# A retention stage with gelu's table loaded earlier, gelu in halves, and three more fixed places in the engines' queues

## The chip, the cores and the metric

One core of a Trainium2 chip runs the kernel. The metric is the device time in microseconds, from several runs; beside them stands one execution taken by the hardware profiler, whose trace has every instruction of the engines (TensorE or PE, its weight loads PEld, VectorE or DVE, ScalarE or ACT, GpSimd or POOL, SyncE or SP) with start and duration. Times inside the trace are counted from the start of the span.

## The reference

A trunk of two layers on x of 1 x 1024 x 1024 in float32. Layer 0 projects the normed x once and feeds an S5 branch and a retention branch; layer 1 is a convolution module.

```python
# layer 0
u_s5, g_s5, q, k, v, g_ret = split(rmsnorm(x) @ w_in)
y = gelu(s5(u_s5)); y = y * sigmoid(y @ glu_w + glu_b)       # S5 branch with its GLU
y_s5 = y * silu(g_s5)
y_ret = retention(rope(q) / 8, rope(k), v) * silu(g_ret)     # 8 heads, normed per head
x = x + concat(y_s5, y_ret) @ w_out
# layer 1
a, b, g = split(rmsnorm(x) @ w_in_c)
u = layernorm(conv31(a * sigmoid(b)))
x = x + (silu(u) * silu(g)) @ w_out_c
return rmsnorm(x)
```

## The kernel before

Everything is held transposed: 128 rows of features by tokens, the 1024 tokens in two halves h of 512. A float32 product is made of three matmuls (`mm3`, L224): each operand is split into a high part, rounded to fp32r, and a low part, the rest. Weights pass through `wload_pieces` (L209): a DMA on SP loads wf, ScalarE casts it to wh (L220), GpSimd or VectorE subtracts to get wl (L221). Each of the three has three buffers, and `wnext` (L162) asks for two weights ahead of the one in use. Some weights are used twice; their low part is then stored and loaded again (`wload_again`, L191).

The order of the instructions on each engine isn't that of the program text. The kernel is built with a timeline planned ahead: an instruction takes its place on its engine when the plan sees its operands ready and the engine free, and the one traced first has precedence. The engines then run these queues strictly in order; SP's queue of DMA issues too. Three means set the order by hand: `issue_after(ins)` puts the instructions of a block behind `ins` on the engine of `ins`; `at(priority)` changes the precedence; and the pairs of `ORDER` (L41) and `s5_order` (L49) put one named instruction behind another on one engine. A pair ('DVE', ('kraw_3', 0), ('yn_2', 0)) reads: on VectorE, the first instruction that writes kraw_3 stands behind the first that writes yn_2.

Retention (`retention`, L1077) goes over four pairs of heads. For each, `ret_proj` projects k and q on PE (mm_k, mm_q) and turns them: four DMAs swap rows of 32 into swp, GpSimd makes two products for each half (L1158, L1160), VectorE adds them (L1161). V comes from `ret_values_wide` for pairs 0 and 1 together (PE mm_v, L1216 to L1218, eight weights v0_0_0 to v0_1_3 in the order h, j, whose low halves GpSimd makes) and from `ret_values` for pairs 2 and 3: eight blocks, each in one of three PSUM banks and copied from there by ScalarE (L1195). `ret_heads` then makes the scores, the state and the output, and norms it per head: VectorE's statistics, a root on ScalarE (`last_rs`, L530, four for each pair), the reciprocal.

Beside each pair k, `y_pass` (L1027) takes two blocks of the S5 branch's output y through gelu: it loads yt (tile yp, one buffer), ScalarE computes the gelu of 128 x 1024 into yn, reading yt with a stride (L1038), SP stores yn, and VectorE forms sums and differences of its quadrants (L1046 to L1049) and splits them for the GLU, whose product is made of seven smaller ones. From pair 1 on the gelus stand behind the last root of the pair before; in pair 2 also behind the copies of V's third and last blocks. `glu_sums` (L1058) forms the same sums of the GLU's weights in the buffers swp and raw that retention frees, and stores them. The root's function and gelu are in different activation tables of ScalarE, so a table load stands between them; in the kernel before nothing names it, and it appears in the trace ahead of the activation that needs it (L1038, L530).

The GLU follows in `layer0_back_and_layer1` (L1343): products mm_glu on PE, and for each block a VectorE operation into a spare bank (mm_gluy, L1460, for half 0; mm_gluz, L1477, for half 1), then `gated` (L1403): tanh on ScalarE in that bank, and VectorE's multiplication with yg (L1421), the second operation on mm_gluy or mm_gluz. For half 1 the bank that L1477 reads is then the target of the next product (y22). After this come w_out (mm_wo, with yr0 and yr1 loaded and split by `load_split`), layer 1's products, its convolution (VectorE's taps, L1626) and w_out_c (mm_oc, `w_out_c`, L1770). There, blocks 0, 1 and 2 of half 1 begin while the normed and gated z comes row block by row block from `conv_scale`. Each such block is 24 matmuls into one bank, three for each row block: number 0 is high by high of row block 0, number 2 the first that needs the weight's low part, number 6 the first that needs row block 2.

Of the kernel before, what the change touches and what calls it, by code (L numbers as in the profile page):

```python
# [14 lines left out]
AF = mybir.ActivationFunctionType  # L15
# [4 lines left out]
P = 128  # L20
# [21 lines left out]
    ('DVE', ('kraw_3', 0), ('yn_2', 0)),  # L42
    ('SP', ('gs1_3', 0), ('t_d', 7)),
    ('DVE', ('cv6_0', 23), ('h1l0_1', 0)),
    ('Pool', ('qswp_0', 0), ('wl_v0_0_1', 0)),
)


# [53 lines left out]
class Trunk:  # L102
# [924 lines left out]
    def y_pass(self, rp, k):  # L1027


        nc = self.nc  # L1030
        yns = []
        for i, cb in enumerate((k, k + 4)):
            yt = rp.tile([P, 8, P], F32, name=f"yp_{cb}", tag="yp", bufs=1)
            nc.sync.dma_start(yt[:], self.y_d[cb].rearrange("i h g m -> (h g) i m"))
            yn = rp.tile([P, P, 8], F32, name=f"yn_{cb}", tag="ynt", bufs=2)

            with self.tc.issue_after((self.last_v if i else self.third_v).ins) if k == 2 else nullcontext():
                nc.scalar.activation(yn[:], yt[:].rearrange("p i m -> p m i"), AF.Gelu_apprx_tanh)  # L1038
            yn = yn[:].rearrange("p m i -> p (m i)")
            nc.sync.dma_start(self.yn_d[cb * P:(cb + 1) * P], yn)  # L1040
            yns.append(yn)
        (b11, b12), (b21, b22) = ((y[:, :HALF], y[:, HALF:]) for y in yns)
        v = nc.vector
        yield
        with self.tc.issue_after(self.last_raw.ins):
            v.tensor_tensor(b22, b22, b12, op=ALU.subtract)  # L1046
            v.tensor_tensor(b12, b12, b11, op=ALU.subtract)
            v.tensor_tensor(b11, b22, b11, op=ALU.add)
            v.tensor_tensor(b21, b11, b21, op=ALU.subtract)  # L1049
        yield  # L1050
        for i in range(2):
            hi = rp.tile([P, T], F32R, name=f"th{i}_{k}", tag="yp", bufs=1)
            v.tensor_copy(hi[:], yns[i])
            v.tensor_tensor(yns[i].bitcast(F32R), yns[i], hi[:].bitcast(F32), op=ALU.subtract)
            nc.sync.dma_start(self.t_d[i, 0, k * P:(k + 1) * P], hi[:].bitcast(F32))
            nc.sync.dma_start(self.t_d[i, 1, k * P:(k + 1) * P], yns[i])
# [20 lines left out]
    def retention(self, st):  # L1077
        nc, A = self.nc, self.A
        rp = self.rp = self.pool("ret", 1, stack=st)
        early = ExitStack()  # L1080
        rq = self.rq = self.pool("retq", 1, stack=early, side="right")
        self.rk = rq.tile([P, 2, T], F32, name="ropek")
        nc.sync.dma_start(self.rk[:], A["rope_k"])
        self.g128 = rp.tile([P, 4], F32, name="g128")
        nc.sync.dma_start(self.g128[:], A["ret_g128"])
        ahead = None
        for pair in range(4):
            cur = list(ahead or self.ret_proj(pair))[-1]

            ahead = pair == 1 and self.ret_proj(pair + 1)  # L1090
            if ahead:
                next(ahead)
            for g, tag in (((0, "swp"), (1, "raw")), (), ((3, "raw"),), ())[pair]:
                self.glu_sums(g, tag)
            if pair == 0:
                V = self.ret_values_wide()
            elif pair > 1:
                V = self.ret_values(pair)
            with ExitStack() as held:
                if pair:  # L1100
                    held.enter_context(self.tc.issue_after(self.last_rs.ins))
                parts = self.y_pass(rq, pair)
                next(parts)
                if pair != 2:
                    next(parts)
                if pair in (0, 3):
                    next(parts, None)

            def scored():

                if pair == 2:
                    with self.tc.issue_after(self.masked[0].ins):
                        next(parts)

            def turned():
                if pair == 3:
                    early.close()
                    self.lp = self.pool("l1", side="right")
            self.ret_heads(pair, *cur, V, turned, scored)

            if pair < 3:
                with self.tc.issue_after((self.ons[0] if pair in (1,) else self.masked[1]).ins):
                    if pair == 0:
                        self.glu_sums(2, "swp")
                    else:
                        next(parts, None)
# [892 lines left out]
```

## Time and profile before

| | before |
|---|---|
| device time, median of 3 runs | 1135.58 us (1133.12 to 1136.41) |
| profiled execution | 1138.03 us |
| its span in the trace | 1136.2 us |
| retention with y's gelus | about 317 to 560 us |
| GLU of S5 | about 529 to 627 us |
| w_out_c of half 1 | from about 1081 us |
| granted TensorE clock, mean | 0.999 |

A timeline row has start, duration, engine, line, operation, output <- input, shape and count; in brackets the idle time of the engine before it and what ended it. A row with x2 or x3 merges neighbours, its duration from the first's start to the last's end. A row of waits has the total, how often, and the longest. PE rows of one matmul are about 0.4 us long but follow each other every 0.2, since matmuls are pipelined.

### The profile page before, as it was taken

What the parts mean: (1) busy time and instruction counts of PE and PEld (TensorE: products, weight loads), DVE (VectorE), ACT (ScalarE), POOL (GpSimd) and SP (SyncE); (2) the same over time, 40 slices, a digit from 0 to 9 for tenths busy, and PEclk for the clock granted to TensorE, in tenths of its full rate; (3) what the DMA queues carried; (4) which work ended last, traced back from release to release, by engine and by line L of the source; (5) the groups of instructions that cost most, each with busy time, mean ns of one, the idle gap of its engine ahead of it and who ended that gap; (6) DMA issues with size and microseconds to landing.
All of it is one profiled execution on the core that took longest, in us unless ns stands there. A gap on an engine that the chain in (4) does not pass through costs nothing.

```text
span 1136.2 us, 17205 instructions
## 1 busy us (share of the span) xinstructions
PE 1117.1 (98%) x6278; PEld 978.9 (86%) x6278; DVE 828.1 (73%) x1470; ACT 498.0 (44%) x731; POOL 647.3 (57%) x456
## 2 busy tenths in 40 slices
PE   9999999999999999999999999999999999999997
PEld 7888888888888889898888888888888888888886
DVE  6973966777417469587569632599999899999734
ACT  6412433333223221323436523555535677446773
POOL 2059999888127344232475011589544568779863
PEclk9999999999999999999999999999999999999999
DMA  9345555553477866959998998565778755357965
GB/s 354 114 124 167 188 185 176 177 172 138 151 245 251 303 212 181 337 168 325 382 372 277 328 330 285 192 237 198 242 252 281 249 195 179 119 179 246 317 229 187
DMA packets 118181, 262.51 MB, mean 231 GB/s; under 512 B 10704, under 2 KB 42320, under 8 KB 117456
## 3 DMA queue, kind: packets, MB, share of 16 engines
q1 hardware_dynamic: 114640, 248.82, 64.9%
q10 hardware_dynamic: 3456, 12.58, 2.8%
q8 instruction: 49, 0.80, 0.3%
q14 instruction: 36, 0.29, 0.1%
HBM read 182.53 MB, written 74.65 MB: 226 GB/s over the span
## 4 chain that ended last, share of the span: by engine, by line
PE 73%; DMA 13%; DVE 7%; ACT 3%; issue 2%; POOL 1%; SPq 1%; POOLq 0%; DVEq 0%; ACTq 0%
PE mm_g L231 7%; PE mm_g L232 7%; PE mm_g L233 7%; PE mm_wo L231 5%; PE mm_wo L233 5%; PE mm_wo L232 5%; PE mm_a L233 2%; DMA yp<-y_d 2%; PE mm_b L232 2%; PE mm_a L231 2%; PE mm_b L233 2%; PE mm_a L232 2%; PE mm_b L231 2%; PE mm_oc L233 2%; PE mm_oc L231 2%; PE mm_oc L232 2%
## 5 line engine op out<-in xcount | busy, mean ns | idle before, releaser
L1626 DVE SCALAR_TENSOR_TENSOR cv<-u,convw,cv 128x512 f32<-128x512 f32 x390 | 267.7, 749 | 5.4 <-ACT cv L1593 3.4
L1587 POOL TENSOR_TENSOR tp<-tp,tp 128x512 f32<-128x512 f32 x64 | 82.4, 1288 | 33.8 <-ACT tp L1586 32.9
L231 PE MATMUL mm_g<-xh,wh_g 128*128 128x512 f32 x256 | 97.9, 382 | 0.0
L232 PE MATMUL mm_g<-xl,wh_g 128*128 128x512 f32 x256 | 97.0, 379 | 0.0
L233 PE MATMUL mm_g<-xh,wl_g 128*128 128x512 f32 x256 | 95.7, 379 | 0.0
L492 POOL TENSOR_TENSOR s1q<-s1q,s1q 128x512 f32<-128x512 f32 x12 | 17.1, 1424 | 79.1 <-ACT s1q L487 79.1
L1586 ACT ACTIVATE tp<-u,convw 128x512 f32<-128x512 f32 x64 | 45.3, 718 | 34.4 <-POOL tp L1587 33.6
L231 PEld LDWEIGHTS mm_g<-xh,wh_g 128*128 128x128 f32 x256 | 48.8, 191 | 6.8 <-issue 0.2
L442 DVE TENSOR_TENSOR gt<-mm_g,R 128x512 f32<-128x512 f32 x32 | 21.9, 686 | 44.7 <-PE mm_g L233 44.6
L233 PEld LDWEIGHTS mm_g<-xh,wl_g 128*128 128x128 f32 x256 | 48.4, 189 | 6.9
L232 PEld LDWEIGHTS mm_g<-xl,wh_g 128*128 128x128 f32 x256 | 48.4, 189 | 6.6
L221 POOL TENSOR_TENSOR wl_glu<-wf_glu,wh_glu 128x1024 fp32r<-128x1024 f32 x14 | 34.0, 2432 | 33.1 <-ACT wh_glu L220 33.1
L233 PE MATMUL mm_oc<-zh,wl_woc 128*128 128x512 f32 (+1 forms) x144 | 51.0, 357 | 1.2 <-DMA wl_woc<-lo_woc 1.2
L232 PE MATMUL mm_oc<-zl,wh_woc 128*128 128x512 f32 (+1 forms) x144 | 51.2, 356 | 0.0
L231 PE MATMUL mm_oc<-zh,wh_woc 128*128 128x512 f32 (+1 forms) x144 | 50.7, 363 | 0.0
L232 PE MATMUL mm_u<-xl,wh_u 128*128 128x512 f32 x128 | 48.3, 381 | 0.7 <-DVE xl L365 0.7
L233 PE MATMUL mm_a<-h1h,wl_ca 128*128 128x512 f32 x128 | 48.6, 380 | 0.3 <-DMA wl_ca<-lo_ca 0.3
L231 PE MATMUL mm_wo<-ysh,wh_wos 128*128 128x512 f32 x128 | 48.9, 382 | 0.0
L231 PE MATMUL mm_g<-h1h,wh_cg 128*128 128x512 f32 x128 | 48.9, 382 | 0.0
L232 PE MATMUL mm_wo<-ysl,wh_wos 128*128 128x512 f32 x128 | 48.5, 379 | 0.0
L233 PE MATMUL mm_wo<-ysh,wl_wos 128*128 128x512 f32 x128 | 48.5, 379 | 0.0
L233 PE MATMUL mm_b<-h1h,wl_cb 128*128 128x512 f32 x128 | 48.5, 379 | 0.0
(533 smaller groups left out, 3601.9 us busy)
## 6 DMA issues: line engine op xcount, KB each, us to landing
wf_g<-w_ab SPq DMA_DIRECT2D x16, 512.0 KB, 5.0
wf_wos<-w_out SPq DMA_DIRECT2D x16, 512.0 KB, 4.5
wf_wor<-w_out SPq DMA_DIRECT2D x16, 512.0 KB, 5.6
wf_cb<-w_c SPq DMA_DIRECT2D x16, 512.0 KB, 4.8
wf_ca<-w_c SPq DMA_DIRECT2D x16, 512.0 KB, 5.6
wf_woc<-w_out_c SPq DMA_DIRECT2D x16, 512.0 KB
wf_v<-w_v SPq DMA_DIRECT2D x12, 512.0 KB
wf_cg<-w_c SPq DMA_DIRECT2D x11, 512.0 KB, 4.5
```

Source lines behind the costliest of these rows:

```text
L221: self.low_made = lo[i].tensor_tensor(wl[:].rearrange(fl)[:, c], wf[:, c], h.bitcast(F32), op=ALU.subtract)
L231: nc.tensor.matmul(ps, wh[:, kb, :], xh, start=start, stop=False, **more)
L232: nc.tensor.matmul(ps, wh[:, kb, :], xl, start=False, stop=False, **more)
L233: self.last_mm = nc.tensor.matmul(ps, wl[:, kb, :], xh, start=False, stop=stop, **more)
L442: nc.vector.tensor_tensor(nat(gt[:, c]), un(ps[:]), nat(self.R[:, c]), op=ALU.mult)
L492: nc.gpsimd.tensor_tensor(a, a, sq[:], op=ALU.add)
L1586: nc.scalar.mul(sk[:], u[:, k:k + HALF], cw[:, nb, k:k + 1])
L1587: gp.tensor_tensor(s0[:], s0[:], sk[:], op=ALU.add)
L1626: v.scalar_tensor_tensor(dst[:], *tap, accs_[i][:], op0=ALU.mult, op1=ALU.add)
```

## The change

Five edits. The pair on GpSimd puts the first product of pair 0's swapped q (L1160, qswp_0) behind the low half of weight v0_1_0 instead of that of v0_0_1, which is three weights later. A new pair on PE puts the third matmul of mm_oc2_1_0 (w_out_c, block 2, half 1) behind the seventh of mm_oc0_1_0. A new pair on VectorE puts the second operation on mm_gluy3 (L1421) behind the first on mm_gluz0 (L1477). For pairs 1, 2 and 3 a load of gelu's table is issued behind the last root of the pair before. And in these pairs each gelu of 128 x 1024 becomes two, for output columns 0 to 63 and 64 to 127 of the outer index (512 elements each).

```diff
@@ ORDER
-    ('Pool', ('qswp_0', 0), ('wl_v0_0_1', 0)),
+    ('Pool', ('qswp_0', 0), ('wl_v0_1_0', 0)),
+    ('PE', ('mm_oc2_1_0', 2), ('mm_oc0_1_0', 6)),
+    ('DVE', ('mm_gluy3', 1), ('mm_gluz0', 0)),
 )
@@ y_pass
             with self.tc.issue_after((self.last_v if i else self.third_v).ins) if k == 2 else nullcontext():
-                nc.scalar.activation(yn[:], yt[:].rearrange("p i m -> p m i"), AF.Gelu_apprx_tanh)
+                for m in ((slice(0, 64), slice(64, P)) if k in (1, 2, 3) else (slice(0, P),)):
+                    nc.scalar.activation(yn[:, m], yt[:, :, m].rearrange("p i m -> p m i"), AF.Gelu_apprx_tanh)
@@ retention
                 if pair:
                     held.enter_context(self.tc.issue_after(self.last_rs.ins))
+                    nc.scalar.preload_act_table_set("gelu_apprx_tanh_and_others")
                 parts = self.y_pass(rq, pair)
```

## The prediction

> **What bounds the kernel now.** I read the page first, then the waits of TensorE (PE) from 300 to 660 us, then the timelines of the engines around each wait.
>
> ```profile
> PE 1117.1 (98%) x6278; PEld 978.9 (86%) x6278; DVE 828.1 (73%) x1470; ACT 498.0 (44%) x731; POOL 647.3 (57%) x456
> ...
> PE 73%; DMA 13%; DVE 7%; ACT 3%; issue 2%; POOL 1%; SPq 1%; POOLq 0%; DVEq 0%; ACTq 0%
> ```
>
> PE is busy 98% of the span and carries 73% of the chain that ended last. So the end moves only by what PE's idle gaps gain or lose. Between 300 and 660 us these are its waits (columns: total us, times, longest):
>
> ```profile
> PE mm_glu L231 <- ACT sg L1416: 1.6, 1, 1.6
> PE mm_v L1217 <- POOL wl_v L221: 1.5, 2, 1.2
> PE mm_v L1192 <- ACT v L1195: 1.1, 1, 1.1
> PE mm_glu L231 <- ACT v L1195: 0.9, 1, 0.9
> PE mm_wo L231 <- ACT yr0h L1339: 0.9, 1, 0.9
> PE mm_glu L231 <- DVE mm_gluz L1477: 0.7, 1, 0.7
> PE mm_k L233 <- POOL wl_k L221: 0.6, 1, 0.6
> ```
>
> The five edits each stand at one such gap: the GpSimd place at mm_v <- wl_v (1.2), the table and the halves at the two gaps <- ACT v (1.1 and 0.9), the VectorE place at mm_gluz (0.7), the TensorE place at one more gap near the end (1.2, shown below). Together that is 5.2 us, the most that the gaps aimed at can give. The three others (sg, yr0h, wl_k) are not touched and can take gains back, since PE will reach them earlier.
>
> **The change part by part.**
>
> *1. GpSimd: the q swap multiplies behind the low half of v0_1_0.*
>
> ```profile
> 350.46 2.51 POOL L1160 TENSOR_TENSOR qswp<-qswp,ropeq 128x512 f32<-128x512 f32 x2 [1.40 <-DMA gs<-w_glu]
> ```
>
> ```profile
> 352.93 8.36 POOL L221 TENSOR_TENSOR wl_v<-wf_v,wh_v 128x1024 fp32r<-128x1024 f32 x3
> ```
>
> ```profile
> 348.72 1.05 ACT L220 CAST wh_v<-wf_v 128x1024 fp32r<-128x1024 f32 x1 [1.15 <-issue]
> ```
>
> GpSimd stood idle 1.40 us, from 349.06, waiting for the swapped q, then spent 2.51 on it, and only at 352.93 began the low halves that PE was about to need: three in 8.36, of which the first (v0_0_3) is PE's wait of 1.2. Its cast and that of v0_1_0 (ended 349.77) were done. Put ahead, two lows run from 349.06 at about 2.4 each, so that v0_0_3 is ready near 351.5 and the 1.2 goes. What moves back: two multiplies, from 350.46 to about 353.8, and with them the q additions on VectorE, the load of gs into the buffer that they free, and what stands behind that load in SP's in-order queue, up to the next K weights:
>
> ```profile
> 351.77 4.51 DVE L1161 TENSOR_TENSOR qrot<-qrot,qswp 128x512 f32<-128x512 f32 x2 [6.12 <-POOL qswp L1160]
> 356.20 2.87 DVE L1046 TENSOR_TENSOR yn<-yn,yn 128x512 f32<-128x512 f32 x1
> ```
>
> ```profile
> 362.37 0.68 DVE L1048 TENSOR_TENSOR yn<-yn,yn 128x512 f32<-128x512 f32 x1
> ```
>
> ```profile
> 372.78 1.11 SPq L218 DMA_DIRECT2D wf_k<-w_ab  x1
> ```
>
> The same kind of VectorE operation takes 0.68 alone and 2.87 where a GpSimd operation runs beside it, so it is held for some 2.2. I walk the queue by that: swaps from 353.8 to 356.4, the q additions done near 357.6 instead of 356.28 (351.77 + 4.51), so 1.4 later; then the sums of y and gs, of which one or two fewer meet a low half (2.2 to 4.4 saved) but which wait for the later gs load (1.4) and may meet the next low half instead (2.2 lost). The chain ends between 2 us earlier and 0.7 later. The wf_k load at 372.78 stands in SP's queue behind the stores of those sums, and PE already waits 0.6 for its low half, so what PE has won is kept only as far as wf_k comes earlier. Ends: 1.8 (the 1.2 and the 0.6 both go) and minus 0.7. I take **1.0**, nearer the upper end, because buffers for weights also come free sooner as the low halves end sooner.
>
> A rule that speaks against this edit: GPSIMD Engine Reference of the Trainium skill (section 1, Specifications) says that GpSimd's SBUF interfaces are shared with VectorE, with contention for VectorE instructions that have two SBUF inputs. The trace agrees (0.68 alone, 2.87 beside GpSimd). By the rule alone the delayed additions and sums meet whatever low halves are left, the first rival, and the sum would be 2.3 instead of 4.0.
>
> *2. The table behind the preceding pair's last root; gelu in halves.* In pair 1 nothing is to be had, since the load already follows the root at once (405.33):
>
> ```profile
> 404.75 0.56 ACT L530 ACTIVATE rs<-mv,epst 128x4 f32<-128x4 f32 x2
> 405.33 1.28 ACT L1038 ACT_TABLE_LOAD   x1
> ```
>
> In pair 2 it isn't so:
>
> ```profile
> 456.49 0.47 ACT L1195 ACTIVATE v<-mm_v,Rtok 128x256 f32<-128x256 f32 x1 [2.21 <-PE mm_v L1194]
> ```
>
> ```profile
> 460.40 0.47 ACT L1195 ACTIVATE v<-mm_v,Rtok 128x256 f32<-128x256 f32 x1 [3.43 <-PE mm_v L1194]
> 465.84 1.28 ACT L1038 ACT_TABLE_LOAD   x1 [4.97 <-DMA yp<-y_d]
> 467.14 1.98 ACT L1038 ACTIVATE yn<-yp 128x1024 f32<-128x1024 f32 x1
> 469.02 1.19 ACT L1195 ACTIVATE v<-mm_v,Rtok 128x256 f32<-128x256 f32 x3
> ```
>
> ```profile
> 469.53 0.38 PE L1192 MATMUL mm_v<-wh_v,xh 128*128 128x256 f32 x1 [1.13 <-ACT v L1195]
> ```
>
> ScalarE copied V block 3 (460.40), then waited 4.97 for yp, loaded the table (1.28), ran the gelu (1.98), and only then copied three finished blocks. PE has three banks for them and stood 1.13. With the table loaded before, the gelu begins at 465.84. Two halves cost a little more than one: a 1024-wide cast is 1.05 (348.72) and a 512-wide one 0.57 (1083.10, below), so 0.09 per cut, six cuts on ScalarE, which is 44% busy. The stores of yn stay one per block, so no DMA is added. The copies then start near 467.9 (465.84 + 1.98 + 0.09) instead of 469.02, or near 466.9 if one is placed between the halves. The wait falls to 0.1 or to nothing: **1.05**, ends 1.13 and minus 1.6 (the third rival). Unhidden, the table load has only been moved: where it now runs, ScalarE is waiting for V blocks (2.21 idle before 456.49). If a copy stood right behind it there, it would be up to 1.28 late, still less than the slack of two free banks at 2.68 (2.21 + 0.47) each.
>
> In pair 3:
>
> ```profile
> 498.68 0.56 ACT L530 ACTIVATE rs<-mv,epst 128x4 f32<-128x4 f32 x2 [3.96 <-DVE mv L1316]
> 500.15 1.28 ACT L1038 ACT_TABLE_LOAD   x1 [0.91 <-DMA yp<-y_d]
> 501.44 2.05 ACT L1038 ACTIVATE yn<-yp 128x1024 f32<-128x1024 f32 x1
> 508.69 2.05 ACT L1038 ACTIVATE yn<-yp 128x1024 f32<-128x1024 f32 x1 [5.21 <-DMA yp<-y_d]
> ```
>
> ```profile
> 528.39 0.62 ACT L1339 CAST y21h<-y21f 128x512 fp32r<-128x512 f32 x1 [6.08 <-DMA y21f<-yn_d]
> 528.92 0.83 ACT L1195 ACTIVATE v<-mm_v,Rtok 128x256 f32<-128x256 f32 x2
> ```
>
> ```profile
> 529.44 0.48 PE L231 MATMUL mm_glu<-y11h,wh_glu 128*128 128x512 f32 x1 [0.94 <-ACT v L1195]
> ```
>
> The roots end at 499.24, yp is there at 500.15. The load can run from 499.24 to 500.52, so the first gelu begins 0.92 earlier, less 0.09 for the cut. The second yp is loaded into the buffer that the first gelu frees, then come the second gelu, yn, y11, y21, and y21's cast (528.39) ahead of the two copies for which PE waits 0.94. All of this is one chain of DMA and engines with little idle time of its own, so the 0.8 arrives: **0.8**, ends 0 (y21 held elsewhere) and 0.94.
>
> *3. VectorE: mm_gluz0 ahead of mm_gluy3's second operation.*
>
> ```profile
> 599.20 0.69 DVE L1425 SCALAR_TENSOR_TENSOR ysl<-mm_gluy,ysh 128x512 fp32r<-128x512 f32 x1
> 600.09 0.70 DVE L1421 SCALAR_TENSOR_TENSOR mm_gluy<-mm_gluy,yg 128x512 f32<-128x512 f32 x1 [0.20 <-ACT mm_gluy L1416]
> 600.70 0.69 DVE L1477 TENSOR_TENSOR mm_gluz<-gu,mm_glu 128x512 f32<-128x512 f32 x1
> ```
>
> ```profile
> 610.00:620.00 10.00, 10.00 (x48) 8.77 (x47) 10.00 (x11) 5.04 (x9) 4.41 (x3) 1.00 0.82 276
> ```
>
> The product into that bank waits for the addition that ends at 601.39. From 599.89 VectorE was free for it, so it ends near 600.5 and the 0.7 goes; the displaced operation comes 0.4 later, and so do what it feeds on ScalarE and the buffer it frees for a yg load. Some 25 us on, PE waits 0.9 for yr0h, whose loads need VectorE, full in that stretch (10.00 of 10). PE's lead may be spent there. Ends 0.72 and minus 0.4; I take **0.4**.
>
> *4. TensorE: the third product of mm_oc2 behind the seventh of mm_oc0.*
>
> ```profile
> 1083.10 0.57 ACT L1339 CAST zh<-zz 128x512 fp32r<-128x512 f32 x1
> ```
>
> ```profile
> 1085.31 0.48 PE L233 MATMUL mm_oc<-zh,wl_woc 128*128 128x512 f32 x1 [1.24 <-DMA wl_woc<-lo_woc]
> ```
>
> PE is held at 1085.31 by the low weights of block 2, while z of row block 2 is there since 1083.67 (its low part some 0.7 later). Products of blocks 0 and 1 with it can run first, at 0.21 each (48 in 10.00). One is certain, two are likely (0.43), all six would fill 1.24. Ends 0.2 and 1.24, **0.75** taken. Behind the pinned product only products of PE queue, and all are wanted before the same bank reads.
>
> The sum: 1.0 + 1.05 + 0.8 + 0.4 + 0.75 = **4.0 us**. The profiled execution took 1138.03 (span 1136.2, 1.8 around it), so it would become 1134.0. It lies 2.45 above the median of 1135.58; brought to that median, the forecast is **1131.6**.
>
> **The rivals.**
>
> *First edit given back at K.* The additions are held behind other low halves and wf_k leaves 0.7 later. Against it: fewer operations stand beside GpSimd. Sum 4.0 minus 1.7 = 2.3: **1133.3**.
>
> *Slower: the same hold, twice more.* Place: VectorE between 353.8 and 372, before SP's wf_k. Price: 2.2 for each further operation held. With two, wf_k leaves 0.7 + 4.4 = 5.1 later and PE's lead elsewhere (3.0) doesn't pay for it: 2.1 slower, **1137.7**. It decides from wf_k 3.0 later, 375.8 in today's times. For it: all of this is in one in-order queue. Against it: GpSimd has then fewer low halves left.
>
> *The table edit doesn't do what it says.* The order of each queue is planned ahead, and the plan misjudged yp by the 4.97 above. If the gelu is planned ahead of block 3's copy, or the load lands in front of the gelu again, part 2 gives nothing or less: without them 4.0 minus 1.85 = 2.15, **1133.4**; with block 3 blocked too, PE stops a block (2.68) sooner and, the copies coming 1.1 sooner, the gap grows by 1.6 instead of falling by 1.05: 4.0 minus 2.65 = 1.35, **1134.2**.
>
> **How the numbers follow.** Forecast 0.60 (its own range 1130.0 to 1133.2), given back at K 0.15, table edit without effect 0.13, slower by the hold 0.12. The range goes from 1129.8 (all 5.2 and the 0.6 at K) to 1135.6, and leaves out the slower case and tails. About 0.3%, 3.4 us, is what a measurement of this kernel can tell from no change, so faster needs below 1132.2: some 0.75 of the forecast and a little of the rest, 0.47. Slower needs above 1139.0: the far half of the hold and an order worsened elsewhere, 0.09. Same 0.44.
>
> **What would show it.** Right: PE's waits on wl_v (1.2), on ACT v (1.1 and 0.9), on mm_gluz and on wl_woc gone or under 0.5; a table load directly behind the roots before 456 and at 499. Wrong: a wait at mm_k above 1.5 (first edit), a PE gap near 466 instead of 469 (gelu ahead of block 3), yr0h above 1.3 (VectorE's place spent), wl_woc still above 0.8. A new wait after 660, where today PE has only one above 0.6, would mean that the planned order moved where no edit stands.

## The result and the profile after

| | before | changed |
|---|---|---|
| median of 22 executions | 1134.56 us (1131.82 to 1138.12) | 1139.32 us (1132.17 to 1143.27, and one of 1672.59) |
| ratio, 95% interval | | 1.0032 (1.0020 to 1.0044) |
| profiled execution | 1138.03 us, span 1136.2, clock 0.999 | 1140.96 us, span 1139.2, clock 0.996 |

The change made the kernel 0.32% slower; the forecast was 0.35% faster. One execution of the changed kernel (1672.59 us at a mean clock of 0.752) was disturbed and is left out of the comparison. The ratio lies between that of the means (1.0029) and that of the medians (1.0041) of the executions compared. The other 21 lie in two groups: 6 from 1132.17 to 1134.61, all at a clock of 0.998 or 0.999, and 15 from 1136.01 to 1143.27, all but one at 0.996 or 0.997.

The page of the changed kernel, busy time and the chain that ended last:

```profile
PE 1121.4 (98%) x6278; PEld 983.4 (86%) x6278; DVE 827.2 (73%) x1470; ACT 498.0 (44%) x737; POOL 646.5 (57%) x456
...
PE 76%; DMA 10%; DVE 6%; ACT 3%; issue 2%; SPq 1%; POOL 1%; POOLq 0%; DVEq 0%; ACTq 0%
```

TensorE is still the bound, but its busy time grew by 4.3 us for the same 6278 instructions. So matmuls became longer. About 2.8 us of it were lost at K (worked out below). The rest is spread over the span: in this execution a product of mm_g<-xh,wl_g took 380 ns on average, against 379 before and in the further profiles of the changed kernel. Its waits (total us, times, longest; the lines of the code have moved by 2 to 4):

```profile
PE mm_k L233 <- ACT wh_k L222: 3.0, 1, 3.0
PE mm_v L1221 <- POOL wl_v L223: 1.9, 2, 1.0
...
PE mm_glu L233 <- ACT v L1199: 0.6, 1, 0.6
...
PE mm_glu L235 <- POOL wl_glu L223: 0.5, 1, 0.5
PE mm_oc L235 <- DMA wl_woc<-lo_woc: 0.5, 1, 0.5
PE mm_v L1196 <- ACT v L1199: 0.4, 1, 0.4
```

The waits at which the other four edits (parts 2 to 4 of the prediction) aimed shrank: ACT v from 1.1 and 0.9 to 0.4 and 0.6, wl_woc from 1.2 to 0.5, mm_gluz from 0.7 to nothing. New are 3.0 at the first product of K and 0.5 at wl_glu. The wait on wl_v, at which the first edit aimed, didn't shrink (1.5 before, 1.9 now).

What happens at K, TensorE's timeline and its clock in steps of 2 us (columns: stretch, length, busy time of PE, PEld, DVE, ACT, POOL with counts, granted clock, DMA share, GB/s):

```profile
382.53 0.60 PE L1240 MATMUL ktp<-ident,krot 128*128 128x128 f32 x4
386.16 0.80 PE L233 MATMUL mm_k<-xh,wh_k 128*128 128x512 f32 x1 [3.03 <-ACT wh_k L222]
...
389.18 0.63 PE L233 MATMUL mm_k<-xh,wh_k 128*128 128x512 f32 x1
```

```profile
384.00:386.00 2.00, 0.00 (x0) 0.00 (x0) 1.92 (x3) 0.94 (x1) 0.00 (x0) 0.79 1.13 343
386.00:388.00 2.00, 1.84 (x6) 1.32 (x6) 0.10 (x1) 2.00 (x5) 1.82 (x1) 0.50 1.04 402
388.00:390.00 2.00, 1.70 (x4) 1.17 (x4) 0.59 (x1) 1.36 (x2) 1.10 (x2) 0.50 1.05 375
390.00:392.00 2.00, 2.00 (x6) 1.60 (x5) 0.00 (x0) 0.00 (x0) 1.78 (x1) 0.51 0.56 168
```

TensorE stands 3.03 us, and behind that the clock is at 0.50 for about 6 us: a product takes 0.63 instead of 0.38. The busy time of the last three rows, 5.54, at half speed is 2.8 us lost. In the kernel before every window from 370 to 395 has a clock of 1.00.

Why K's weights come late is read from four queues. GpSimd:

```profile
342.65 1.72 POOL L1162 TENSOR_TENSOR qrot<-qraw,ropeq 128x512 f32<-128x512 f32 x1
...
351.84 1.28 POOL L1164 TENSOR_TENSOR qswp<-qswp,ropeq 128x512 f32<-128x512 f32 x1 [1.83 <-DMA yn_d<-yn]
353.07 5.13 POOL L223 TENSOR_TENSOR wl_v<-wf_v,wh_v 128x1024 fp32r<-128x1024 f32 x2
358.17 1.72 POOL L1164 TENSOR_TENSOR qswp<-qswp,ropeq 128x512 f32<-128x512 f32 x1
```

Only one of the two swap products has moved behind the low halves; the pair names one instruction, and the other still stands ahead of them. VectorE:

```profile
353.15 2.83 DVE L1165 TENSOR_TENSOR qrot<-qrot,qswp 128x512 f32<-128x512 f32 x1 [8.23 <-POOL qswp L1164]
...
371.54 0.69 DVE L1056 CAST th<-yn 128x1024 fp32r<-128x1024 f32 x1 [1.39 <-DMA t_d<-th]
372.15 0.69 DVE L1165 TENSOR_TENSOR qrot<-qrot,qswp 128x512 f32<-128x512 f32 x1
```

The second addition of q is now placed behind both casts of y and ends at 372.84; before, both were done at 356.28. It frees the buffer qswp for the next load of gs. The load of ropeq needs only GpSimd's products, which ended at 359.89, but its place in SP's queue is now behind the first stores of t_d and ws_d. SP's queue:

```profile
370.80 1.49 SPq L1139 DMA_DIRECT2D ropeq<-rope_q  x1
372.38 1.21 SPq L1058 DMA_DIRECT2D t_d<-th  x1
373.68 0.78 SPq L1068 DMA_DIRECT2D gs<-w_glu  x1
374.55 0.74 SPq L1059 DMA_DIRECT2D t_d<-yn  x1
375.38 0.45 SPq L220 DMA_DIRECT2D wf_k<-w_ab  x1
```

The same loads in the kernel before, and the sizes of two of them (the view of DMA issues; gs, t_d and ws_d have 512 KB too):

```profile
353.00 0.34 SPq L1135 DMA_DIRECT2D ropeq<-rope_q  x1
356.31 0.55 SPq L1065 DMA_DIRECT2D gs<-w_glu  x1
```

```profile
ropeq<-rope_q SPq DMA_DIRECT2D x1, 1024.0 KB
wf_k<-w_ab SPq DMA_DIRECT2D x2, 512.0 KB
```

So 1.5 MB whose loads had been issued 16 and 20 us ahead of that of K's weights now stand right in front of it. The cast of K's weights in the changed kernel, and then in the kernel before, there with GpSimd's last product of q and the first transposes behind V as well:

```profile
385.06 1.04 ACT L222 CAST wh_k<-wf_k 128x1024 fp32r<-128x1024 f32 x1 [10.09 <-DMA wf_k<-w_ab]
```

```profile
380.10 1.05 ACT L220 CAST wh_k<-wf_k 128x1024 fp32r<-128x1024 f32 x1 [6.79 <-DMA wf_k<-w_ab]
```

```profile
343.36 1.74 POOL L1158 TENSOR_TENSOR qrot<-qraw,ropeq 128x512 f32<-128x512 f32 x1
```

```profile
381.57 0.60 PE L1236 MATMUL ktp<-ident,krot 128*128 128x128 f32 x4
```

Counted from that product of q (343.36 and 342.65), which makes executions comparable, the cast began at 36.7 before and at 42.4 in the changed kernel, and V ended, where the transposes ktp begin, at 38.2 and 39.9. The transfer, from the issue to the cast, took 7.3 and 9.7.

### The profile page after: what moved, and what is told of

It reads as the page before. It is cut to its first block, busy times and chain, and to the rows that moved or that the text cites. A ratio compares the mean times of both kernels' runs of the same rounds, so it can differ in the third digit from the quotient of the medians.

```text
span 1139.2 us, 17213 instructions
## 1 busy us (share of the span) xinstructions
PE 1121.4 (98%) x6278; PEld 983.4 (86%) x6278; DVE 827.2 (73%) x1470; ACT 498.0 (44%) x737; POOL 646.5 (57%) x456
## 4 chain that ended last, share of the span: by engine, by line
PE 76%; DMA 10%; DVE 6%; ACT 3%; issue 2%; SPq 1%; POOL 1%; POOLq 0%; DVEq 0%; ACTq 0%
PE mm_g L233 7%; PE mm_g L234 7%; PE mm_g L235 7%; PE mm_wo L235 5%; PE mm_wo L234 5%; PE mm_wo L233 5%; DMA yp<-y_d 3%; PE mm_b L234 2%; PE mm_b L235 2%; PE mm_a L235 2%; PE mm_a L233 2%; PE mm_a L234 2%; PE mm_b L233 2%; PE mm_oc L235 2%; PE mm_oc L234 2%; PE mm_oc L233 2%
## 5 line engine op out<-in xcount | busy, mean ns | idle before, releaser
L233 PE MATMUL mm_b<-h1h,wh_cb 128*128 128x512 f32 x128 | 48.6, 380 | 0.0
```

The source lines that it names most:

```text
L233: nc.tensor.matmul(ps, wh[:, kb, :], xh, start=start, stop=False, **more)
```

## The experiments

Theory: the whole loss is the first edit, by the bytes that it puts ahead of K's weights, and the idle time then halves the clock; the other four edits win about what was forecast. The rival put first was that one of the other edits costs it.

### Which edit

**e1_old_pool_pin**, the changed kernel without the first edit:

```diff
-    ('Pool', ('qswp_0', 0), ('wl_v0_1_0', 0)),
+    ('Pool', ('qswp_0', 0), ('wl_v0_0_1', 0)),
```

> The changed kernel with the first edit alone undone (the GpSimd product is pinned ahead of block 0_1 of V again; table, halves and the other two pins stay). My theory: all of the loss comes from the first edit, through the load of K's weights, and the other four edits win about what was forecast. Then TensorE's wait at the first product of K falls from 3.0 to under 0.8 us, the granted clock of 380 to 395 us is 1.00, and the time is 2 to 3.5 us below the kernel before (ratio 0.997 to 0.998). Rival: the other edits cost it (the table load or the halves disturb the order); then the time stays at or above the kernel before, and the wait at K stays over 2.

Measured: 1132.72 us, ratio 0.9995 (0.9981 to 1.0009). The 3.0 at K is gone, and what is left there is 0.4 at wl_k; the clock is 1.00. So the loss is the first edit's. But the gain of the other four is some 0.6 us (-1.0 to 2.2) and not the 2 to 3.5 expected: this half of the theory isn't borne out.

**e2_pool_pin_alone**, the kernel before with the first edit alone:

```diff
-    ('Pool', ('qswp_0', 0), ('wl_v0_0_1', 0)),
+    ('Pool', ('qswp_0', 0), ('wl_v0_1_0', 0)),
```

> The kernel before with the first edit alone. My theory: TensorE waits 2.5 to 3.5 us at K's first product, the clock falls to about 0.5 behind it, and the time is 4 to 8 us above the kernel before, with the executions in two groups if the clock falls in only some of them; the waits on ACT v (1.1 and 0.9), mm_gluz (0.7) and wl_woc (1.2) stay as before. Rival (the other edits cost it): within 2 us of the kernel before, wait at K at most 1.

Measured: 1136.82 us (1133.62 to 1142.05), ratio 1.0025 (1.0010 to 1.0040); 3.4 us at K and a clock of 0.50 behind it. The wait, the clock and the side are as expected; the size, 2.8 us, is below the 4 to 8; the further profiles of the changed kernel suggest that not every execution waits so long (below).

**e7_table_and_halves**, the kernel before with the table load and the halves, and none of the three pairs in `ORDER`:

```diff
-                nc.scalar.activation(yn[:], yt[:].rearrange("p i m -> p m i"), AF.Gelu_apprx_tanh)
+                for m in ((slice(0, 64), slice(64, P)) if k in (1, 2, 3) else (slice(0, P),)):
+                    nc.scalar.activation(yn[:, m], yt[:, :, m].rearrange("p i m -> p m i"), AF.Gelu_apprx_tanh)
...
+                    nc.scalar.preload_act_table_set("gelu_apprx_tanh_and_others")
```

> The kernel before with the table load behind the roots and gelu in two halves, and none of the three pins. Forecast of the prediction: 1.85 us below the kernel before (ratio 0.9984), the waits of V's products and of the first glu product on ACT v (1.13 and 0.94) under 0.3 together. Theory A (the profiled waits are larger than the usual ones): 0 to 1 us below, ratio 0.999 to 1.000. Rival (the table load now lies on a path): above the kernel before, with a wait on ACT v over 1.5.

Measured: 1132.58 us, ratio 0.9987 (0.9973 to 1.0001), so 1.5 us faster, with an interval that just reaches no change. The first of the two waits on ACT v is 0.6, the second under 0.2, together more than the 0.3 of the forecast. The time is near the forecast of the prediction.

**e9_vector_pin_alone**, the kernel before with the pair on VectorE:

```diff
+    ('DVE', ('mm_gluy3', 1), ('mm_gluz0', 0)),
```

> The kernel before with the third edit alone (VectorE: mm_gluz0 ahead of the second operation on mm_gluy3). My theory, from the profiles so far: the wait of the first product of y22 on mm_gluz (0.5 to 1.0 in three profiles of the kernel before) goes, and instead the first product of yt1 waits 0.4 to 1.3 for the low half of its weights, some 3 us later; net 0, ratio 0.9993 to 1.0007. Forecast of the prediction: 0.4 us won, ratio 0.9996, and the lead spent at yr0h; then no wait on wl_glu over 0.2.

Measured: 1135.26 us, ratio 1.0011 (1.0000 to 1.0022). Its waits:

```profile
PE mm_glu L234 <- POOL wl_glu L222: 0.7, 1, 0.7
...
PE mm_glu L232 <- DVE mm_gluz L1478: 0.5, 1, 0.5
```

The wait on wl_glu is in all eight profiles with this pair and without filling (0.2 to 1.3) and in none without the pair; of the four filled ones (below) only e3 has it (0.8). It stands some 4 us behind the wait at which the pair aims, and that one is 0.5 here and at most 0.2 in the seven others. The gain is given back at once; that the ratio is on the slow side is at the edge of what can be told.

**e11_table_halves_tensor_pin**, the edits of e7 and the pair on TensorE:

```diff
+    ('PE', ('mm_oc2_1_0', 2), ('mm_oc0_1_0', 6)),
```

> The kernel before with the table load, the halves and the TensorE pin: the two edits (2 and 4) for which the profiles show a gain that isn't given back at once. By the waits in the profiles so far 1.0 and 0.4 us: ratio 0.9985 to 0.999, below both kernels; the wait on wl_woc under 0.6, the two waits on ACT v under 0.8 together. If the gains of edit 2 were chance, the ratio is 0.9997 to 1.0005.

Measured: 1131.95 us, ratio 0.9987 (0.9974 to 1.0000); wl_woc 0.3, the waits on ACT v 1.1 together, more than expected. This is the lowest median of all, and the version that comes out of the study: the changed kernel with the old pair on GpSimd and none on VectorE, 0.13% below the kernel before, with an interval that reaches no change, where the changed kernel is 0.32% above it.

### What the first edit does

**e4_k_weights_first**, the changed kernel with two more places on SP's queue:

```diff
+    ('SP', ('ropeq_1', 0), ('wf_k1', 0)),
+    ('SP', ('gs1_0', 0), ('wf_k1', 0)),
```

> The changed kernel, the GpSimd pin included, with two more places on the loads' queue: the table ropeq of the next pair (1 MB) and the second half of gs (0.5 MB) behind K's weights. My theory, that these 1.5 MB ahead of K's weights make the wait: K's weights leave by 373 and take about 7 us, the wait at K's first product is under 0.8, the clock stays at 1.00, and the time is 1130.5 to 1133.5. Rival, the forecast's own slower case (VectorE's held operations delay the queue ahead of K's weights): they still leave after 375, the wait stays above 1.5, the time above 1136.

Measured: 1133.59 us, ratio 0.9996 (0.9981 to 1.0011), waits at K 0.7, clock 1.00; the median is 0.1 us above the expected range. SP's queue and the cast:

```profile
372.30 0.99 SPq L222 DMA_DIRECT2D wf_k<-w_ab  x1
373.34 1.06 SPq L1070 DMA_DIRECT2D gs<-w_glu  x1
374.45 0.64 SPq L1141 DMA_DIRECT2D ropeq<-rope_q  x1
```

```profile
378.97 1.04 ACT L224 CAST wh_k<-wf_k 128x1024 fp32r<-128x1024 f32 x1 [6.17 <-DMA wf_k<-w_ab]
```

With the GpSimd pair in place and GpSimd and VectorE in the order of the changed kernel, the transfer takes 6.7 (372.30 to 378.97) once the 1.5 MB follow instead of preceding. That shows the mechanism, and it answers the prediction's slower rival: counted from GpSimd's product of q, the load leaves at 30.2, no earlier than in two of three profiles of the changed kernel (28.1 and 28.8, table below); it is only no longer queued behind the others.

**e10_both_products_moved**, the changed kernel and the second product pinned too:

```diff
+    ('Pool', ('qswp_0', 1), ('wl_v0_1_0', 0)),
```

> The changed kernel with both products of the q turn placed behind the low halves of blocks 0_3 and 1_0, as the prediction walked it. If the failure was that only one of the two moved, the wait at K falls under 1 us and the time is below the kernel before. My theory: it is the order of the loads behind it, the 1.5 MB of ropeq and gs ahead of K's weights, which stays; then K's weights leave after 374.5, the wait at K is 2 to 4 us, and the ratio 1.002 to 1.005, as with one product moved.

Measured: 1133.81 us, ratio 0.9998 (0.9986 to 1.0009); 1.2 us at K, on wl_k. My theory expected 2 to 4 us and a loss, and fell here. SP's queue:

```profile
366.81 1.05 SPq L1140 DMA_DIRECT2D ropeq<-rope_q  x1
...
370.59 0.60 SPq L1069 DMA_DIRECT2D gs<-w_glu  x1
371.28 0.77 SPq L221 DMA_DIRECT2D wf_k<-w_ab  x1
```

Nearly the same loads and stores stand ahead, but they are spread out. From the first store of t_d on, 4.5 MB are issued ahead of K's weights in both: in 10.3 us here (360.96 to 371.28), where the load of gs waits for an addition that took 2.85 on VectorE and ended at 370.56, and in 7.6 in the changed kernel (367.83 to 375.38). At the 0.4 MB per us that the full queue moves (343, 402 and 375 GB/s in the rows of the changed kernel from 384 to 390) 4.5 MB take 11.3. That leaves a backlog, as an estimate, of 3.7 us in the changed kernel, of 1.8 in the kernel before (3 MB in 5.7), and of 2.3 here (0.9, and 1.4 for a pause in which the queue had run empty ahead of 364.87). The transfers were 9.7, 7.3 and 7.8. So what decides isn't the order alone but how many bytes are still waiting when K's load is issued.

The other profiles bear this out but for e8 (estimates worked out in the same way, us):

| profiles | backlog when K's load is issued | transfer |
|---|---|---|
| e7, e9 | none | 5.0, 4.9 |
| e4 | 1.0 | 6.7 |
| e8 | 1.5 | 8.3 |
| before, e1, e5, e6, e11 | 1.8 | 6.8 to 7.3 |
| e10 | 2.3 | 7.8 |
| changed, e2, e3, e12 to e16 | 3.6 to 4.3 | 9.7 to 11.0 |

The profiles e7 and e9 also answer the slower rival. K's load left there at 31.8 and 31.5 counted from the product of q, 2 us later than in e5 and e6 and later than in every profile with one product moved but the first (32.7). Yet the cast began at 36.7 and 36.4, as in the kernel before, since by the estimate the queue was empty by then.

The Trainium skill says in DMA: Bandwidth & Descriptors (Queues, rings and completion order) that on each DMA engine the descriptors of a ring are consumed in ring order; the traces agree (9.7 with the 1.5 MB ahead, 6.7 in e4 with them behind).

**e8_old_pin_k_first**, the other four edits and K's weights first:

```diff
-    ('Pool', ('qswp_0', 0), ('wl_v0_1_0', 0)),
+    ('Pool', ('qswp_0', 0), ('wl_v0_0_1', 0)),
+    ('SP', ('ropeq_1', 0), ('wf_k1', 0)),
+    ('SP', ('gs1_0', 0), ('wf_k1', 0)),
```

> Edits 2 to 5 without the first edit, and K's weights placed ahead of the table ropeq and of the second half of gs. If K's weights are late in the kernel before as well (its product waited 0.6 for their low half), this wins that too: wait at K under 0.3, 1.0 to 1.5 us below the kernel before, ratio about 0.999, the best of these. Rival: ropeq and gs, now behind, come late to the next pair's turn of q and to the sums of the glu; then a new wait of over 1 us after 395, and the time is at or above the kernel before.

Measured: 1134.30 us, ratio 1.0003 (0.9987 to 1.0019). K waits for nothing (its cast begins 4.5 us ahead of V's end), and yet no gain over the kernel before is shown: the profile has 1.4 on ACT v instead.

### The idle time and the clock

**e3_idle_filled** and **e12_idle_filled_to_the_end**, the changed kernel with N = 13 and N = 20 products that nobody reads:

```diff
+            for _ in range(N if (pair, hf) == (0, 0) else 0):
+                nc.tensor.matmul(ps[:], self.ones_r[:], self.xs[0][0][0][:], start=True, stop=True)
             for b in range(4):
                 t0 = (4 * hf + b) * P
```

> The changed kernel with 13 products of 128x512 that nobody reads, put on TensorE between the last product of V and the transposes of K, where it stood idle; their bank is overwritten by the transposes. 13 at 0.22 are 2.8 us, about the idle time; the weights of K arrive as late as before. If it is the idle of 3 us that trips the clock, the clock stays at 1.00 through 380 to 395, the executions form one group, and the time is that of the faster group of the changed kernel, 1132 to 1135, below the median of 1139.3 by 4 to 7. Rival: the clock falls by itself or by the traffic; then the 0.5 stays at 386 to 392 and the time stays near 1139, or rises.

Measured: 1138.15 us, ratio 1.0046 (1.0029 to 1.0064). The expectation missed. V ended earlier in the profiled execution, the filling ran out at 382.87, and two shorter waits were left:

```profile
379.68 3.19 PE L1239 MATMUL ktp<-xh,ones_r 128*128 128x512 f32 x13
...
384.42 0.66 PE L1242 MATMUL ktp<-ident,krot 128*128 128x128 f32 x4 [1.12 <-ACT v L1224]
...
386.27 0.69 PE L235 MATMUL mm_k<-xh,wl_k 128*128 128x512 f32 x1 [0.76 <-POOL wl_k L223]
```

The clock fell to 0.50 all the same. It takes no single long wait: 1.88 us of idle time within the 3.0 from 383.3 to 386.3 were enough.

> As the earlier run with 13 products of 128x512, but 20 of them, 4.3 us, so that TensorE is busy until K's weights are there. There two shorter waits (1.12 and 0.76 within 3.2 us) were left, and the clock fell to 0.5. If idle time within some microseconds trips it, no wait over 0.8 is left at K, the clock stays at 1.00 from 380 to 395, no execution is at 0.996, and the time is 1.5 to 3 us below the changed kernel, 1135.5 to 1137.5, because K's weights are as late as before. Rival (something else trips it): the clock falls again and the time is 1139 or more.

Measured: 1137.37 us, ratio 1.0037 (1.0021 to 1.0052). The filling, K's cast and the clock at K, with no wait there:

```profile
379.64 4.83 PE L1239 MATMUL ktp<-xh,ones_r 128*128 128x512 f32 x20
```

```profile
382.05 1.05 ACT L222 CAST wh_k<-wf_k 128x1024 fp32r<-128x1024 f32 x1 [11.33 <-DMA wf_k<-w_ab]
```

```profile
385.00:390.00 5.00, 5.00 (x27) 3.96 (x26) 1.23 (x2) 2.02 (x3) 2.93 (x2) 1.00 0.85 293
```

K's cast began 2.4 us behind V's end (382.05 against 379.64), as late as in the changed kernel (2.5), and the same loads stood ahead of it in SP's queue. So it is TensorE's idle time that trips the clock: filled, it stays at 1.00. This rests on the one profile, since the mean clock of an execution doesn't tell (two of the 12 are at 0.997, and the profiled executions of e2 and e3, with a fall, at 0.998). Filling saves nothing all the same (ratio 1.0037 against 1.0032); the likely reason, not tested, is that the 20 products take 4.3 us in the executions too in which K's weights aren't late.

### How executions differ

**e5_before_again** and **e6_before_third**, the kernel before, unchanged:

> The kernel before, unchanged, for a second profile. Theory A: the waits that edits 2 to 5 take away are partly of the one profiled execution (1138.03, which is 3.5 us over the median of all executions); then the four waits (ACT v 1.13 and 0.94, mm_gluz 0.72, wl_woc 1.24: 4.03 in all) come to 2 us or less here, and the gap is in other places or missing. Rival B: they stand in every execution; then they come to 3.5 us or more, and the gain of the four edits is lost to new waits.

> The kernel before, unchanged, for a third profile. Theory A: the same four waits come to 2 us or less, with other sizes than in the second profile. Rival B: 3.5 us or more.

Measured: 1132.93 and 1133.81 us. The waits of the first of them at the places of the edits:

```profile
PE mm_v L1192 <- ACT v L1195: 1.7, 2, 0.9
PE mm_oc L233 <- DMA wl_woc<-lo_woc: 1.3, 1, 1.3
...
PE mm_glu L231 <- DVE mm_gluz L1477: 0.5, 1, 0.5
...
PE mm_v L1217 <- POOL wl_v L221: 0.2, 1, 0.2
PE mm_glu L231 <- ACT v L1195: 0.2, 1, 0.2
```

The waits at which the other four edits aim come to 3.7 here and 3.4 in the third profile (0.6, 1.3, 1.0, 0.5), against 4.0: theory A (2 or less) is wrong, they recur, though each is different every time and the third profile lies just under the 3.5 of rival B. But the wait on wl_v, the first edit's target of 1.2, is 0.2 here and under 0.2 in the third: it belonged to one execution.

**e13_after_again** and **e14_after_third**, the changed kernel, unchanged:

> The changed kernel, unchanged, for a second profile. Theory C (the groups are the clock gate): if this execution is below 1135, the wait at K is under 2 us or is split, and the clock from 380 to 395 is 1.00; if it is above 1137, the wait is over 2.5 and the clock falls to 0.5. Rival D (the groups come from the load of K's weights, longer in some executions, the clock only follows): the time from the start of q's product on GpSimd to the cast of K's weights differs between the groups by 3 us or more (42.4 in the first profile).

> The changed kernel, unchanged, for a third profile, with the same two theories: C, the distance from q's product to the cast of K's weights is 40 to 43 us in every execution and only the clock differs; D, it is under 39 in an execution below 1135.

Measured: 1134.00 and 1131.76 us. At K:

```profile
380.39 0.48 PE L233 MATMUL mm_k<-xh,wh_k 128*128 128x512 f32 x1 [0.36 <-ACT wh_k L222]
...
382.83 0.48 PE L235 MATMUL mm_k<-xh,wl_k 128*128 128x512 f32 x1 [0.98 <-POOL wl_k L223]
```

Counted from GpSimd's product of q (worked out from the same four rows of each trace as above):

| execution | K's load issued | K's cast | transfer | V's end | cast behind V's end |
|---|---|---|---|---|---|
| before, 1138.03 | 29.4 | 36.7 | 7.3 | 38.2 | -1.5 |
| before, e5, 1132.93 | 29.3 | 36.4 | 7.2 | 38.1 | -1.6 |
| before, e6, 1133.81 | 29.6 | 36.4 | 6.8 | 38.4 | -2.0 |
| changed, 1140.96 | 32.7 | 42.4 | 9.7 | 39.9 | +2.5 |
| changed, e13, 1134.00 | 28.8 | 39.7 | 11.0 | 39.9 | -0.1 |
| changed, e14, 1131.76 | 28.1 | 38.5 | 10.4 | 39.9 | -1.4 |
| first edit alone, e2 | 30.8 | 41.4 | 10.6 | 38.5 | +2.9 |
| K's weights first, e4 | 30.2 | 36.9 | 6.7 | 38.2 | -1.4 |
| both products, e10 | 31.3 | 39.1 | 7.8 | 39.8 | -0.7 |

This is theory D in the main: the cast is 2.7 and 3.9 us earlier in the two faster executions, where D set 3. In every profile of the one-product order, e4 with its other order of loads apart, the transfer is 9.7 to 11.0 us instead of 7. Whether it hurts depends on how late K's load leaves (28.1 to 32.7), which varies from one execution to the next. Why is only in part seen: ScalarE began the second gelu of pair 0 2.0 us behind the start of q's product in the first profile (344.62) and within 0.1 of it in the others (339.52 and 339.20), but only 0.5 behind it in e2, where the load left late too. Before, the cast was 1.5 to 2.0 us ahead of V's end; the first edit spends that slack and up to 3 us more. From about 1.9 us of idle time within some 3 us on, the clock can fall as well, which adds 1.4 (e2), 1.6 (e3) or 2.8 us (changed kernel), estimates from the busy time at the lower clock. So 1140.96 against 1134.00 and 1131.76 is mostly a threshold at K, and the clock follows. That all of the two groups come from it isn't shown: the 12 executions of the filled kernel e12 lie in two groups as well, 7 from 1135.13 to 1137.41 and 5 from 1140.29 to 1142.15, and no profile fell in the upper one.

**e15_filled_again** and **e16_filled_third**, the kernel of e12 once more:

> The kernel with 20 products in TensorE's idle time, for a second profile. Its 12 executions had 7 from 1135.1 to 1137.4 and 5 from 1140.3 to 1142.2, nearly all at a mean clock of 0.998 or 0.999. C: no execution of it should be above 1138 without a fall of the clock. D: an execution above 1140 shows K's weights or another load 3 to 5 us later than the 39.7 of the first profile, with the clock at 1.00.

> The same for a third profile: below 1138 with K's cast at 39 to 41 us behind q's product and the clock at 1.00, or above 1140, and then the waits of TensorE tell where the 5 us are: at K (D), or in a stage behind it (neither).

Measured: 1139.02 and 1134.73 us, both with the clock at 0.999, K's cast at 39.3 and 39.5 and no wait at K. So the 4.3 us between these two aren't K's: TensorE's waits behind K add up to 4.7 in the slower one (1.6 on ACT v, 1.0 at the retention's output products, smaller ones) and to 2.5 in the other. That is about half of the 4.3 us; where the rest is stays open. Theory C (nothing above 1138 without a fall of the clock) is wrong.

## Why the prediction was wrong

**The step that failed is the first edit.** The prediction put it: "What moves back: two multiplies, from 350.46 to about 353.8, and with them the q additions on VectorE, the load of gs into the buffer that they free, and what stands behind that load", and "the chain ends between 2 us earlier and 0.7 later". Its own sign of that came: a wait at mm_k above 1.5 (3.0). Four things in it were wrong.
- The pair names one product, so one moved. Its addition didn't come 1.4 later but 16.6 (356.28 to 372.84), since the plan placed it anew behind the casts of y.
- Of the queue behind it, gs was named but not ropeq, twice as large and also waiting for the swap products. They went from 356.31 and 353.00 to 373.68 and 370.80, in front of the very load that the prediction watched.
- Only the issue of K's load was followed, not its transfer. Against the means of the three profiles before (29.4 and 7.1), the issue moved by -1.3 to +3.3 in the four profiles with one product moved and nothing else changed at K; the transfer grew by 2.6 to 3.9 in each.
- The gain at wl_v was read from one execution: over the unfilled profiles it is 0.53 without the edit (eight) and 0.58 with it (six).

The edit alone costs 2.8 us (1.1 to 4.5, from e2) where 1.0 was to be won. The forecast's slower rival had the place right, the queue ahead of K's weights, but not the mechanism: it priced held VectorE operations, and e4 shows that the loss goes with only the loads put in another order. Its point (375.8; measured 375.38) was met by luck, since in two further profiles the load left earlier than before. It had a chance of 0.12.

**The clock was missing** altogether: no price was put on idle time beyond the idle time itself. In the profiled execution 3.3 us of waiting at K cost 2.8 more, by the estimate above.

**The table and the halves were right in kind.** As forecast, the load stands directly behind the roots in both pairs (456.15 behind 455.84 + 0.30, and 504.90):

```profile
456.15 1.28 ACT L1105 ACT_TABLE_LOAD   x1
471.89 2.15 ACT L1041 ACTIVATE yn<-yp 128x512 f32<-128x512 f32 x2 [4.42 <-DMA yp<-y_d]
...
504.90 1.28 ACT L1105 ACT_TABLE_LOAD   x1
```

The two waits on ACT v together are 2.1 on average in the five profiles without it (1.9 to 2.4) and 0.9 in the nine unfilled ones with it (0 to 1.5): 1.1 won of the 1.85 forecast; e7 measured 1.5 (-0.1 to 3.1). What is left follows yp, for which the gelu still waits 4.42.

**VectorE's place** was sized 0.4 with the lead spent at yr0h. mm_gluz fell from 0.87 to 0.09 on average, and wl_glu rose from nothing to 0.74, so the lead is spent some 4 us on, at GpSimd's low half and not at yr0h, and the net is about 0.

**TensorE's place** was right: wl_woc fell from 1.03 (six profiles) to 0.40 (eight), 0.6 against the 0.75 forecast; too small for a time of its own (e11 against e7).

So 4.0 was forecast and -3.6 came (ratio 1.0032). Of the difference of 7.6, 3.8 are the first edit (+1.0 against -2.8) and 2.4 the other four (3.0 against 0.6 in e1), much of it gain that the next queue takes back; the last 1.4 are within the intervals.

## What to carry to other kernels

When an instruction is moved that frees a buffer, list every load that waits for that buffer, with its bytes, and see what stands behind them in the same queue; when a load lands depends on the bytes still queued at its issue, and not only on when it is issued. A pair that fixes one of two twin instructions lets a planner place the other anew, so look at the order that comes out. Take a wait as a target only when a second profile of the same kernel has it too, and look a few microseconds on for the next wait before the gain is counted.

## What was unexpected in the hardware

The clock fell to 0.50 after a wait of 3.03 us (and 3.39 in e2), and also after two waits of 1.12 and 0.76 within 3.0 us in e3; it did not after 1.34 in two waits within 2.8 us (e13) or a single 1.9 (e1). The Trainium skill, TensorE: Matmul & The Clock Gate (Part 1), gives as rule no idle gaps above about 3.4 us, by activity in free-running windows of that length. The runs here don't agree with the rule, since 3.03 in a row was enough, and so were two shorter waits; where windows begin they don't show. The clock stayed at 0.5 for 3.5 (e3) to 5.6 us (changed kernel) after work had begun again.
